# Rotary embedding on one core: batches moved in pairs as 32 KB rows, a lead of one row, another start

## The chip, the cores and the metric

The kernel runs on one core of one Trainium2 chip. Times are device microseconds of the whole execution. The span is the part that the profile covers, from the first instruction to the last; the time is about 1.4 us longer. A run is compared with runs of the kernel before on the same chip and, for the most part, in the same rounds. All ratios are the mean time of one kernel's fast runs over the mean of the other's fast runs, so they are not quite the ratio of the medians quoted beside them. Brackets hold the 95% interval.

## The reference

`x` is 16 batches of 512 rows of 1024 fp32 numbers, a row being 16 heads of 64. Each head is rotated by the row's angles:

```
x1, x2 = x[..., :half_dim], x[..., half_dim:]          # half_dim 32
out = concatenate([x1 * cos - x2 * sin, x1 * sin + x2 * cos], axis=-1)
```

33.55 MB come in and 33.55 MB go out. There is one product with the cosine (t1), one of the swapped halves with the signed sine (t2), and a sum.

## The kernel before

A batch is a tile of 2 MB: 4 rows to each of 128 partitions, so one contiguous run of 16 KB per partition in DRAM. Tiles go through a ring of 40 rows in SBUF. SyncE issues the loads (queue q1), ScalarE the stores (q10). GpSimd computes most t2, VectorE all t1 (into PSUM) and most sums; for three rows in eight, TensorE adds t2 with an identity matmul and ScalarE copies the sum out.

```
RING, LEAD = 40, 2
PE2 = [u % 8 in (1, 3, 6) for u in range(NU)]     # summed by TensorE, copied out by ScalarE
V2 = [u % 8 == 3 for u in range(NU)]              # t2 by VectorE instead of GpSimd
...
xv = x.rearrange("b (p r) d -> b p (r d)", r=R)   # R = 4: 16 KB to a partition
...
# SyncE
for c in range(NC):
    if c * R >= RING:
        sp.wait_ge(sem_out[c - RING // R], 16)
    sp.dma_start(tile(c), xv[c]).then_inc(sem_in[c], 16)
...
# ScalarE
ae.dma_start(out[0, 0:seq:seq // 16, 0, 0:HALF], cos[0:seq:seq // 16, :]).then_inc(sem_touch, 16)   # early write of 2 KB
...
    if r == R - 1:
        if c == 0:
            ae.wait_ge(sem_touch, 16)
        wait_added(ae, u)
        ae.dma_start(ov[c], tile(c)).then_inc(sem_out[c] if c < len(sem_out) else sem_rest, 16)
...
# VectorE: the sum of a row trails its product by LEAD rows
for u in range(NU + LEAD):
    if u < NU:
        mul(u)
    if u >= LEAD and not PE2[u - LEAD]:
        comb(u - LEAD)
```

## Time and profile before

| | before |
|---|---|
| time, median of the first 3 runs | 162.03 us |
| span of the profiled run | 160.6 us |
| packets | 4931, of which 4096 of 16 KB |
| DMA share held by q1 and q10 | 49.6% and 48.9% |
| busy VectorE, GpSimd | 131.6 and 130.5 us |
| last store issued | 153.65 us |

The prediction shows the rows of the page, the windows and the GpSimd timeline. To judge a shorter lead one more view is needed, the groups of VectorE with the waits ahead of them (count, busy us, mean ns; after the last bar the idle time just before, and what ended most of it):

```profile
L229 DVE TENSOR_TENSOR t_ps<-x_sb,tab_ps 128x1024 f32<-128x1024 f32 x64 | 77.3, 1227 | 13.4 <-ACT x_sb L144 11.6
L240 DVE TENSOR_TENSOR x_sb<-t_ps,t_sb 128x1024 f32<-128x1024 f32 x40 | 48.6, 1217 | 0.0
```

VectorE stood still 11.6 us for ScalarE to empty a PSUM buffer. And the timeline of the tail, with the instruction that issues the last store at the end:

```profile
150.07 1.23 DVE L229 TENSOR_TENSOR t_ps<-x_sb,tab_ps 128x1024 f32<-128x1024 f32 x1
...
151.21 2.35 DVE L240 TENSOR_TENSOR x_sb<-t_ps,t_sb 128x1024 f32<-128x1024 f32 x2
152.53 1.02 ACT L144 ACTIVATE x_sb<-t_ps 128x1024 f32<-128x1024 f32 x1 [4.88 <-PE t_ps L169]
153.65 0.34 ACTq L149 DMA_DIRECT2D out_dram<-x_sb  x1
```

The last two sums on VectorE and the copy of row 62, after its detour over TensorE and ScalarE, both ended at 153.55 or 153.56, and the last store was issued 0.1 us later.

### The profile page before, as it was taken

The numbers are of one execution on the slowest core, as the hardware profiler recorded it, in microseconds if no ns is written. First come the engines' busy times: TensorE is split into PE (matmuls) and PEld (weight loads), VectorE is DVE, ScalarE is ACT, GpSimd is POOL, SyncE is SP. The second block draws the span as 40 slices with busy tenths as digits, with TensorE's granted clock in tenths as the row PEclk, the third lists the DMA queues.
The fourth block names the chain that finished last, engine by engine and source line by source line (L and its number), as shares of the span: only waits on it lengthen the run. The fifth ranks groups of instructions, "written<-read, shape, count | busy, mean of one in ns | idle before, by whom it ended". The sixth has DMA issues, their size and how long they took to land.

```text
span 160.6 us, 608 instructions
## 1 busy us (share of the span) xinstructions
PE 85.6 (53%) x102; PEld 26.6 (17%) x102; DVE 131.6 (82%) x116; ACT 26.4 (16%) x27; POOL 130.5 (81%) x62
## 2 busy tenths in 40 slices
PE   6004909358529548538548646756626844545800
PEld 1002302212202202211202211211111210120200
DVE  0079299998899969997899989996999979996920
ACT  3010220220120121121021022022012022202020
POOL 1069999999999999999987997999939989399000
PEclk9999975555855556855556755556755586755585
DMA  4999999999999999999999999999999999999996
GB/s 131 404 457 420 441 432 412 432 420 441 416 445 437 416 441 414 445 428 428 435 420 445 424 428 437 424 437 428 428 437 428 432 432 420 445 428 428 437 416 279
DMA packets 4931, 67.27 MB, mean 419 GB/s; under 512 B 576, under 2 KB 832, under 8 KB 832
## 3 DMA queue, kind: packets, MB, share of 16 engines
q1 hardware_dynamic: 2592, 33.69, 49.6%
q10 hardware_dynamic: 2336, 33.56, 48.9%
q14 instruction: 3, 0.02, 0.0%
HBM read 33.69 MB, written 33.56 MB: 419 GB/s over the span
## 4 chain that ended last, share of the span: by engine, by line
DVE 30%; PE 21%; issue 19%; POOL 15%; ACT 5%; DMA 5%; SPq 0%; DVEq 0%; POOLq 0%
PE t_ps L169 21%; DVE x_sb L240 17%; POOL t_sb L198 15%; DVE t_ps L229 10%; ACT x_sb L144 5%; DMA stage<-in_sin_dram 5%; DVE t_sb L220 3%; SPq L128 0%; SPq L125 0%; ACT s_sb L138 0%; ACT s_sb L139 0%; DVEq L228 0%; DVEq L239 0%; POOLq L117 0%
## 5 line engine op out<-in xcount | busy, mean ns | idle before, releaser
L198 POOL TENSOR_TENSOR t_sb<-x_sb,s_sb 128x1024 f32<-128x1024 f32 x56 | 129.8, 2350 | 17.3 <-ACT s_sb L139 8.2
L169 PE MATMUL t_ps<-t_sb,ident 128*128 128x512 f32 x96 | 82.8, 1015 | 65.7 <-DVE t_ps L229 52.6
L229 DVE TENSOR_TENSOR t_ps<-x_sb,tab_ps 128x1024 f32<-128x1024 f32 x64 | 77.3, 1227 | 13.4 <-ACT x_sb L144 11.6
L240 DVE TENSOR_TENSOR x_sb<-t_ps,t_sb 128x1024 f32<-128x1024 f32 x40 | 48.6, 1217 | 0.0
L169 PEld LDWEIGHTS t_ps<-t_sb,ident 128*128 128x128 f32 x96 | 25.8, 295 | 122.2 <-DVE t_ps L229 87.9
L144 ACT ACTIVATE x_sb<-t_ps 128x1024 f32<-128x1024 f32 x24 | 24.6, 1024 | 119.5 <-PE t_ps L169 119.5
L220 DVE TENSOR_TENSOR t_sb<-x_sb,tab_ps 128x1024 f32<-128x1024 f32 x8 | 9.7, 1210 | 0.0
L207 DVE COPY tab_ps<-stage 128x128 f32<-128x128 f32 x1 | 0.3, 295 | 7.6 <-DMA stage<-in_cos_dram 7.6
L155 PE MATMUL t_ps<-zero 128*128 128x512 bf16 x6 | 2.7, 629 | 1.3 <-DVE zero L203 1.3
L138 ACT ACT_TABLE_LOAD x1 | 1.3, 1283 | 1.5 <-PEq L273 1.5
L138 ACT ACTIVATE s_sb<-stage 128x128 f32<-128x128 f32 x1 | 0.3, 309 | 6.3 <-DMA stage<-in_sin_dram 6.3
L155 PEld LDWEIGHTS t_ps<-zero 128*128 128x128 bf16 x6 | 0.7, 136 | 2.4 <-DVE zero L203 1.2
L203 DVE MEMSET zero<- 128x256 uint32 x1 | 0.3, 272 | 0.9 <-PEq L273 0.9
L180 POOL MEMSET ident<- 128x128 f32 x1 | 0.2, 204 | 0.3 <-POOLq L273 0.3
L182 POOL TENSOR_SCALAR_AFFINE_SELECT ident<-ident 128x128 f32<-128x128 f32 x1 | 0.3, 293 | 0.1
L273 POOL MEMSET const-float32-0.0<- 128x1 f32 x1 | 0.1, 99 | 0.3 <-issue 0.3
L139 ACT ACTIVATE s_sb<-stage 128x128 f32<-128x128 f32 x1 | 0.3, 292 | 0.0
L209 DVE TENSOR_SCALAR tab_ps<-stage 128x128 f32<-128x128 f32 x1 | 0.3, 284 | 0.0
L210 DVE COPY tab_ps<-stage 128x128 f32<-128x128 f32 x1 | 0.3, 283 | 0.0
L273 POOL MEMSET const-bfloat16-1.0<- 128x1 bf16 x1 | 0.1, 102 | 0.0
L273 POOL MEMSET const-uint8-127<- 128x1 uint8 x1 | 0.1, 102 | 0.0
L273 POOL MEMSET const-float32-1.0<- 128x1 f32 x1 | 0.1, 98 | 0.0
## 6 DMA issues: line engine op xcount, KB each, us to landing
x_sb<-in_x_dram SPq DMA_DIRECT2D x16, 2048.0 KB, 54.5
out_dram<-x_sb ACTq DMA_DIRECT2D x16, 2048.0 KB, 16.0
stage<-in_cos_dram SPq DMA_DIRECT2D x1, 64.0 KB, 7.6
stage<-in_sin_dram SPq DMA_DIRECT2D x1, 64.0 KB, 7.3
out_dram<-in_cos_dram ACTq DMA_DIRECT2D x1, 2.0 KB, 6.5
```

The source lines that it names most:

```text
L138: ae.activation(s_sb[:, :, 0, :], sv, COPY, scale=-1.0)
L139: ae.activation(s_sb[:, :, 1, :], sv, COPY).then_inc(sem_s, 1)
L144: ae.activation(xs[:, k, :], t1_ps[:, u % NT1, :], COPY).then_inc(sem_a, 1)
L155: pe.matmul(t1_ps[:, k, b * BANK:(b + 1) * BANK], zero[:, 0:P], zero[:], start=True, stop=True).then_inc(sem_w, 1)
L169: ins = pe.matmul(t1_ps[:, u % NT1, b * BANK:(b + 1) * BANK], ident[:], t2[:, b * BANK:(b + 1) * BANK], start=False, stop=True, skip_group ...
L182: pl.affine_select(out=ident[:], in_=ident[:], compare_op=mybir.AluOpType.is_equal, fill=0.0, base=0, pattern=[[-1, P]], channel_multiplier=1,
L198: pl.tensor_tensor(t2_sb[:, u % NT2, :, :, :], swapped(k), sin_of(s_sb, r), mult).then_inc(sem_p, 1)
L203: ve.memset(zero[:], 0.0).then_inc(sem_z, 1)
L220: ve.tensor_tensor(t2_sb[:, u % NT2, :, :, :], swapped(k), sin_of(s_ps, r), mult).then_inc(sem_d, 1)
L229: ve.tensor_tensor(t1_ps[:, u % NT1, :].rearrange("p (h d) -> p h d", d=HALF), x_sb[:, k, :, :, :].rearrange("p h t d -> p (h t) d"), c_ps ...
L240: ve.tensor_tensor(xs[:, k, :], t1_ps[:, u % NT1, :], t2_sb[:, u % NT2, :, :, :].rearrange("p h t d -> p (h t d)"), add,).then_inc(sem_v, 1)
L273: nc = _bacc.Bacc("TRN2", target_bir_lowering=False, num_devices=1)
```

## The change

The intent is fewer and longer packets. Twelve of the batches move in pairs b and b + 6: partition p holds 8 consecutive rows of one of the two, 32 KB in one run. Two batches at each end stay alone, so that compute starts and ends on small tiles. The pair needs its own cosine and sine tables (two small matmuls with a picking matrix). The lead goes from 2 to 1, three rows at the ends are summed on VectorE instead of TensorE, and two more t2 go to GpSimd. At the start, the first row of the first batch is stored alone, and the early write to `out` is gone.

```diff
-    RING = 40
-    NC = batch
+    FAR = (batch - 4) // 2
+    tiles = [(0, R1), (1, R1)] + [(2 + i, R2) for i in range(FAR)] + [(batch - 2, R1), (batch - 1, R1)]
+    RING = 5 * R2
...
-    PE2 = [u % 8 in (1, 3, 6) for u in range(NU)]
-    V2 = [u % 8 == 3 for u in range(NU)]
+    PE2 = [R1 <= u < NU - R1 and u % R2 in (1, 3, 6) for u in range(NU)]
+    V2 = [tiles[t][1] == R2 and r == V_ROW for t, r in rows]
...
-    LEAD = 2
+    LEAD = 1
...
+        x2 = x.rearrange("b (s r) d -> s b (r d)", r=R2)
+        def in_dram(single, pairs, t, r=0):
+            b, n = tiles[t]
+            return single[b, :, r * dim:] if n == R1 else pairs[:, b:b + FAR + 1:FAR, :]
...
-            ae.dma_start(out[0, 0:seq:seq // 16, 0, 0:HALF], cos[0:seq:seq // 16, :]).then_inc(sem_touch, 16)
...
-                if r == R - 1:
-                    if c == 0:
-                        ae.wait_ge(sem_touch, 16)
+                if u == 0:
                     wait_added(ae, u)
-                    ae.dma_start(ov[c], tile(c)).then_inc(sem_out[c] if c < len(sem_out) else sem_rest, 16)
+                    ae.dma_start(o1[0, :, 0:dim], xs[:, 0, :]).then_inc(sem_out[0], 16)
+                if r == tiles[t][1] - 1:
+                    wait_added(ae, u)
+                    k = u // R2
+                    ae.dma_start(in_dram(o1, o2, t, t == 0), in_sbuf(t, t == 0)).then_inc(sem_out[k] if k < EARLY else sem_rest, 16)
```

## The prediction

> **What bounds the kernel now.** I read the page from the top: which engine is never idle, then what the rest wait for. The busy rows and the DMA queues come first.
>
> ```profile
> span 160.6 us, 608 instructions
> ...
> DMA  4999999999999999999999999999999999999996
> GB/s 131 404 457 420 441 432 412 432 420 441 416 445 437 416 441 414 445 428 428 435 420 445 424 428 437 424 437 428 428 437 428 432 432 420 445 428 428 437 416 279
> DMA packets 4931, 67.27 MB, mean 419 GB/s; under 512 B 576, under 2 KB 832, under 8 KB 832
> ## 3 DMA queue, kind: packets, MB, share of 16 engines
> q1 hardware_dynamic: 2592, 33.69, 49.6%
> q10 hardware_dynamic: 2336, 33.56, 48.9%
> ```
>
> The DMA row is full in every slice but the first and the last. The two queues (q1 loads, q10 stores) together held the 16 engines for 49.6 + 48.9 = 98.5% of the span. No compute engine comes near: VectorE is 82% busy, GpSimd 81%. So the question is the work that the DMA engines have, and the unfilled corners at both ends. The windows view separates corners from middle (the last two columns are the DMA share and GB/s):
>
> ```profile
> 0.00:4.00 4.00, 2.74 (x6) 0.73 (x6) 0.27 (x1) 1.28 (x1) 0.70 (x6) 1.00 0.45 131
> 4.00:24.00 20.00, 5.95 (x8) 2.33 (x8) 12.21 (x14) 2.56 (x4) 14.40 (x7) 0.96 1.01 429
> 24.00:136.00 112.00, 67.18 (x76) 20.48 (x76) 103.08 (x90) 19.46 (x19) 105.72 (x46) 0.58 1.01 430
> 136.00:156.00 20.00, 9.72 (x12) 3.03 (x12) 16.05 (x14) 3.07 (x3) 9.73 (x5) 0.65 1.00 429
> 156.00:160.60 4.60, 0.00 (x0) 0.00 (x0) 0.00 (x0) 0.00 (x0) 0.00 (x0) 0.50 0.71 301
> ```
>
> Loads alone (4 to 24), loads with stores (24 to 136) and stores nearly alone (136 to 156) all run at 429 to 430 GB/s. That equality says the engines' own pace is the limit, not HBM and not the direction. The packet records agree: of the 4096 packets of 16 KB, the median load and the median store both took 611 ns, 26.8 GB/s an engine, 429 on 16.
>
> Is compute a close second? The GpSimd timeline of the last third (start, us, then the wait before in brackets) answers:
>
> ```profile
> 102.73 7.06 POOL L198 TENSOR_TENSOR t_sb<-x_sb,s_sb 128x1024 f32<-128x1024 f32 x3
> 110.05 6.98 POOL L198 TENSOR_TENSOR t_sb<-x_sb,s_sb 128x1024 f32<-128x1024 f32 x3 [0.27 <-DMA x_sb<-in_x_dram]
> 119.78 9.30 POOL L198 TENSOR_TENSOR t_sb<-x_sb,s_sb 128x1024 f32<-128x1024 f32 x4 [2.75 <-DMA x_sb<-in_x_dram]
> 129.49 6.97 POOL L198 TENSOR_TENSOR t_sb<-x_sb,s_sb 128x1024 f32<-128x1024 f32 x3 [0.41 <-DMA x_sb<-in_x_dram]
> 139.21 9.28 POOL L198 TENSOR_TENSOR t_sb<-x_sb,s_sb 128x1024 f32<-128x1024 f32 x4 [2.75 <-DMA x_sb<-in_x_dram]
> ```
>
> From 110 us on GpSimd has caught up and waits for each load. The chain of waits nevertheless names compute (DVE 30%, PE 21%), because it follows the last store back to the sum that fed it. But the last store was issued at 153.65 and its packets ran right behind those of the store before (which ended at 155.1), so the tail had under 1 us of slack and no hole. Compute sets the time only if the change makes that last issue later.
>
> **What the Trainium skill says.** "DMA: Bandwidth & Descriptors", section "Where 436 GB/s comes from": 16 ports of 32 B at 850 MHz, 435.2 GB/s. The trace agrees with that as an asymptote: its packets of 512 B took 27 ns and those of 16384 B 611 ns, so (611 - 27) / 15872 B is 36.8 ps a byte, 27.2 GB/s an engine. The same page, "Why small descriptors are slow (HBM only)", has a fixed cost of some 3 cycles per packet. The trace shows more: 611 - 16384 x 0.0368 = 8.2 ns, and the 4-byte packets took 9 ns by themselves; I use 8.2. Its "Latency and other measured facts" warns of row pitches of large powers of two in HBM (half rate at 4 MiB); the pair's neighbours will be 6 batches, 12 MiB, apart, and no run here shows what that does. Its "The descriptor swizzle" spreads 128 partitions over engines so that each has one memory port; for a pattern of 64 by 2 rows on the DRAM side the page says nothing, and that is my largest doubt.
>
> **The change, part by part.**
>
> 1. *32 KB rows.* Twelve of sixteen batches, three quarters of 4096 packets, go from 16 KB to 32 KB: 3072 packets become 1536. If a 32 KB row is one packet, it takes 32768 x 0.0368 + 8.2 = 1214 ns where two took 1222. Removed per engine: 1536 / 16 x 8.2 ns = 0.79 us, on the bound itself. The bytes stay: 67.1 MB at 435 GB/s is 154.3 us, no version goes below that plus its corners.
> 2. *First row alone.* One store of 2 MB becomes one of 4 KB rows and one of 12 KB rows: 128 packets more, 128 / 16 x 8.2 ns = +0.07 us.
> 3. *No early write to out.* 16 packets of 128 B at 13 ns, one an engine: -0.01 us. Nothing waits visibly for it (it landed in 6.5 us, the first store is issued at 21.8). The first load's packets, up to 1.77 us each, lie beside it; if it disturbed them, up to some 0.7 us might come back (queue 1's mean of 618 ns against 611, times 128 packets per engine, is 0.9 us). I count none.
> 4. *Stores start sooner, then come in lumps of 4 MB.* Row 0 can be summed about 4 us after GpSimd starts at 9.6, so its store is issued near 14 instead of 21.8. Loads filled the engines then anyway: 0. Later, when the store queue is empty, 20 MB of loads stand queued: 0.
> 5. *Work moved between engines.* The order view shows 58 GpSimd products for 56, 43 sums on VectorE for 40, 6 of its own products for 8, 42 matmuls of sums for 48. GpSimd: +2 x 2.35 = +4.7 us, 58 x 2.35 = 136.3 in all. VectorE: 64 + 43 + 6 = 113 instructions for 112, +1.2 us. Neither is on the bound unless the tail slips.
> 6. *Tail.* GpSimd from 9.6 without a stop would end at 145.9. In the kernel before it ended at 148.5 and the last store followed 5.2 us later, since sums trailed by two rows and row 62 went over TensorE (3.5 us) and ScalarE. With a lead of one row and no such detour in the last four rows I allow 2 us. The pair of rows 48 to 55 lands whole, so row 48 comes later: loads end near 138 now, less 4 MB at half rate (19.5 us) gives 118, less what stores in lumps let loads gain early. If compute really starts there at 114 to 118, then 7 + 8 products of 2.35 = 35.3 end at 149 to 153, and the last store is issued at 151 to 155. The deadline from above is 155.1 less the 0.8 us from issue to first packet, 154.3. So expected slack 1 to 3 us, loss expected 0.2.
> 7. *Tables.* Two matmuls, four small copies, three set-up instructions on GpSimd, all before row 8 (near 28 us): 0.
>
> Sum: -0.79 + 0.07 - 0.01 + 0.2 = about -0.5 us on 160.6, hence 160.1. The timed run was 1.4 us above its span (162.04 to 160.6), so 161.5. Since parts 3 and 4 can only give, I shade it to 161.3.
>
> **Rivals.** *Compute becomes the bound at the end.* For: 4.7 us more on GpSimd, whole pairs landing late, sums only one row behind, so VectorE meets GpSimd's latency each row. Against: the lead of two cost waits on ScalarE (11.6 us in 8), since fewer VectorE instructions lay between a product and the reuse of its buffer; a lead of one puts another there. Time if it goes wrong: each us after 154.3 is a us, 162 to 165. *The new pattern runs slower on the engines*, by uneven ports or HBM rows 12 MiB apart: a packet of 1300 ns instead of 1214 costs 96 x 86 ns = 8.3 us, some 170. For: nothing in the profile, only the silence of the skill; against: reads and writes held 611 ns flat in every mixture, so HBM has room. *The rows are cut into 16 KB packets again*: then part 1 is nil, 162.0. *The early write had held up the start*: 160.6.
>
> **Range and chances.** The middle cases span 160.6 to 162.5; the tail rival stretches the upper side, so 160.2 to 163.4. Faster by over 2% means under 158.8: the floor of 154.3 + 1.8 until the first packet + 0.5 after the last + 1.4 is 158.0 with no packet cost and no ragged end, so 0.03. Slower by over 2% needs above 165.3, the engine pattern rival or a badly late tail: 0.09. Within 2%: 0.88.
>
> **What would show it.** Right: some 3,300 packets for 4931, 32 KB ones near 1214 ns, DMA share full from 4 us to the last store, GB/s of 431 to 433 in the middle, the last store issued before 154. Wrong: packets of 32 KB above 1225 ns; a digit under 9 in the DMA row before the last slice (compute late); a first slice well above 131 GB/s (the early write did matter); GpSimd's idle time growing on VectorE instead of on loads.

## The result, and the profile after

The changed kernel took 162.00 us (median of 6 runs, 161.41 to 162.24), the kernel before 162.03: ratio 0.999 [0.9968, 1.0012]. Two repeats gave 0.9997 [0.9979, 1.0015] and 0.9995 [0.9983, 1.0007]. So the forecast gain of about 0.45% did not come. These are the same lines of the page as the prediction shows of the kernel before:

```profile
span 160.8 us, 569 instructions
...
DMA  5999999999899999999999999999999999999994
GB/s 147 403 457 461 426 448 420 390 401 506 363 436 440 467 399 473 424 408 467 424 399 456 448 391 440 473 428 387 493 395 403 428 469 395 489 416 391 440 424 204
DMA packets 3314, 67.26 MB, mean 418 GB/s; under 512 B 368, under 2 KB 624, under 8 KB 752
## 3 DMA queue, kind: packets, MB, share of 16 engines
q1 hardware_dynamic: 1728, 33.69, 49.5%
q10 hardware_dynamic: 1584, 33.56, 48.5%
```

The packets fell from 4931 to 3314 as meant. But q1 and q10 hold the engines for 98.0% of the span, where it was 98.5%, and the last slice moved 204 GB/s where it had moved 279: the work on the engines shrank, and some of it ends later. (The 8 in the DMA row is no hole. A packet that takes 1.2 us is booked as a whole, so neighbouring slices of 4 us gain and lose by it; the packet records have no gap above 15 ns on any engine there.) The windows, with DMA share and GB/s last:

```profile
4.00:24.00 20.00, 2.04 (x4) 1.17 (x4) 14.59 (x14) 1.17 (x4) 14.38 (x7) 1.00 1.03 439
24.00:136.00 112.00, 61.96 (x82) 20.64 (x83) 105.87 (x95) 20.47 (x20) 110.46 (x48) 0.74 1.00 431
136.00:156.00 20.00, 2.53 (x3) 0.44 (x2) 9.43 (x8) 1.02 (x1) 9.27 (x4) 0.59 0.98 421
156.00:160.80 4.80, 0.00 (x0) 0.00 (x0) 0.00 (x0) 0.00 (x0) 0.00 (x0) 0.50 0.57 246
```

The long middle gained, 431 GB/s for 430. The last window lost: a share of 0.57 over 4.80 us, where the kernel before had 0.71 over 4.60. Compute is not the cause. VectorE's group with its wait, and the tail of the timeline:

```profile
L296 DVE TENSOR_TENSOR t_ps<-x_sb,pair_ps 128x1024 f32<-128x1024 f32 x48 | 57.6, 1222 | 2.9 <-ACT x_sb L177 2.9
```

```profile
109.17 25.46 POOL L260 TENSOR_TENSOR t_sb<-x_sb,s_sb 128x1024 f32<-128x1024 f32 x11 [0.17 <-DMA x_sb<-in_x_dram]
138.39 9.27 POOL L260 TENSOR_TENSOR t_sb<-x_sb,s_sb 128x1024 f32<-128x1024 f32 x4 [3.76 <-DMA x_sb<-in_x_dram]
```

```profile
147.77 1.23 DVE L307 TENSOR_TENSOR x_sb<-t_ps,t_sb 128x1024 f32<-128x1024 f32 x1 [1.08 <-POOL t_sb L260]
149.08 0.34 ACTq L185 DMA_DIRECT2D out_dram<-x_sb  x1
```

The wait for ScalarE fell from 11.6 to 2.9 us, GpSimd waits for loads and not for VectorE, and the last store is issued at 149.08, 4.6 us earlier than before. It then stands behind other stores.

So who ends late? In the packet records every transfer ends with 16 packets of 4 bytes, one on each DMA engine. Sorted by time, these packets of the last store show every engine's own end. "Middle" is the median of the 16, "last" the sixteenth:

| kernel | middle engine, us | last engine, us | last minus middle |
|---|---|---|---|
| before | 159.51 | 160.12 | 0.61 |
| after | 158.78 | 160.44 | 1.66 |
| after, first repeat | 158.83 | 160.32 | 1.49 |
| after, second repeat | 158.78 | 160.33 | 1.55 |

The middle engine gained 0.7 us, and the last one lost 0.2 to 0.3. (The mean of the sixteen went from 159.61 to 159.00, 159.07 and 158.96.) The time goes by the last. These are three executions with spans of 160.7 and 160.8; of the 17 runs of the changed kernel two had a span of 160.0, and no trace caught one of those. Where it fell behind can be read in the packet records of the first repeat, by putting packets into 16 back-to-back chains. All extra times here are over what a packet of that length usually takes:

```
engine that ended at 160.32, its packets out of the ordinary:
 55.9 us  queue 14 (instructions), 8 KB, 309 ns, between two data packets
 56.2 us  q1  32 KB  +530 ns  (right behind the instruction packet)
122.1 us  q10 32 KB  +158 ns
125.9 us  q10 32 KB  +490 ns
```

0.31 + 0.53 + 0.16 + 0.49 = 1.49 us, all of its lag. Two kinds of events add up: an instruction fetch that passes through one of the 16 data engines, and some slow packets, near 125 us here; in the two other traces the same engine also had one 440 to 540 ns too long at 95 us.

### The profile page after: what moved, and what is told of

Its sections match the earlier page's. It is cut to its first block, busy times and chain, and to the rows that moved or that the text cites. A ratio compares the mean times of both kernels' runs of the same rounds, so it can differ in the third digit from the quotient of the medians.

```text
span 160.8 us, 569 instructions
## 1 busy us (share of the span) xinstructions
PE 69.3 (43%) x94; PEld 23.0 (14%) x94; DVE 130.2 (81%) x117; ACT 23.9 (15%) x26; POOL 136.4 (85%) x67
## 2 busy tenths in 40 slices
DMA packets 3314, 67.26 MB, mean 418 GB/s; under 512 B 368, under 2 KB 624, under 8 KB 752
## 4 chain that ended last, share of the span: by engine, by line
POOL 25%; PE 21%; DVE 16%; issue 15%; DMA 11%; ACT 3%; SPq 1%; POOLq 0%; DVEq 0%
POOL t_sb L260 25%; PE t_ps L215 21%; DMA x_sb<-in_x_dram 11%; DVE t_ps L296 9%; DVE x_sb L307 7%; ACT x_sb L177 3%; SPq L158 1%; DVE t_sb L289 1%; SPq L161 1%; POOLq L145 0%; POOLq L147 0%; DVEq L306 0%
## 5 line engine op out<-in xcount | busy, mean ns | idle before, releaser
L260 POOL TENSOR_TENSOR t_sb<-x_sb,s_sb 128x1024 f32<-128x1024 f32 x58 | 134.1, 2364 | 10.5 <-ACT s_sb L168 6.5
L215 PE MATMUL t_ps<-t_sb,ident 128*128 128x512 f32 x84 | 64.5, 919 | 62.9 <-POOL t_sb L260 41.4
L296 DVE TENSOR_TENSOR t_ps<-x_sb,pair_ps 128x1024 f32<-128x1024 f32 x48 | 57.6, 1222 | 2.9 <-ACT x_sb L177 2.9
L307 DVE TENSOR_TENSOR x_sb<-t_ps,t_sb 128x1024 f32<-128x1024 f32 x43 | 52.4, 1219 | 2.7 <-POOL t_sb L260 2.5
L177 ACT ACTIVATE x_sb<-t_ps 128x1024 f32<-128x1024 f32 x21 | 21.5, 1024 | 106.2 <-PE t_ps L215 106.2
L215 PEld LDWEIGHTS t_ps<-t_sb,ident 128*128 128x128 f32 x84 | 21.1, 278 | 105.4 <-issue 57.2
L296 DVE TENSOR_TENSOR t_ps<-x_sb,tab_ps 128x1024 f32<-128x1024 f32 x16 | 19.3, 1222 | 4.7 <-DMA x_sb<-in_x_dram 4.7
L289 DVE TENSOR_TENSOR t_sb<-x_sb,tab_ps 128x1024 f32<-128x1024 f32 x6 | 7.3, 1213 | 0.0
L198 PE MATMUL pair_ps<-stage,pick 128*128 128x256 f32 x4 | 2.0, 666 | 5.1 <-DMA stage<-in_sin_dram 5.1
L241 POOL TENSOR_SCALAR_AFFINE_SELECT pick<-pick 128x128 f32<-128x128 f32 x2 | 1.4, 704 | 0.1
```

The costliest lines, as they stand in the source:

```text
L177: ae.activation(xs[:, k, :], t1_ps[:, u % NT1, :], COPY).then_inc(sem_a, 1)
L198: pe.matmul(pair_ps[:, k].rearrange("p c r d -> p (c r d)"), pick[:, k].rearrange("q s b -> q (s b)"), stage[:].rearrange("q c f -> q (c f)"),
L215: ins = pe.matmul(t1_ps[:, u % NT1, b * BANK:(b + 1) * BANK], ident[:], t2[:, b * BANK:(b + 1) * BANK], start=False, stop=True, skip_group ...
L241: pl.affine_select(out=pick[:, k], in_=pick[:, k], compare_op=mybir.AluOpType.is_equal, fill=0.0, base=-k, pattern=[[-2, P // 2], [0, 2]], ...
L260: pl.tensor_tensor(t2_sb[:, u % NT2, :, :, :], swapped(k), over_heads(s_of(t, r)), mult).then_inc(sem_p, 1)
L289: ve.tensor_tensor(t2_sb[:, u % NT2, :, :, :], swapped(k), over_heads(v_ps), mult)
```

## The experiments

There were fifteen runs, all with correct results. The first four asked which part of the change moved the time, the next four what the packets cost and what makes an engine late, the rest looked mostly at the start.

### The changed kernel again

No edit.

> The changed kernel once more, unaltered, for a second trace and five more rounds. In the first trace the DMA work per engine fell by 0.63 us (packet times of both queues summed, 158.19 to 157.56 us), yet the last of the 16 engines ended at 160.45 us against 160.13. Theory S (the slowest engine sets the time, and the change spreads the engines): ratio again 0.997 to 1.001, and the last engine again over 1.2 us behind the middle of the 16. Rival L (that trace's slow engine was bad luck): last engine within 0.8 us of the middle, span near 160.1, ratio 0.995 to 0.997.

162.01 us, ratio 0.9997 [0.9979, 1.0015]; mean span of its runs 160.53. It confirms the result, and its trace the picture of a middle engine that gained and a last one that did not.

### Pairs, but 16 KB rows

```diff
-                sp.dma_start(in_sbuf(t), in_dram(x1, x2, t)).then_inc(sem_in[t], 16)
+                for h in range(tiles[t][1] // R1):
+                    sp.dma_start(in_sbuf(t, h * R1, R1), in_dram(x1, x2, t, h * R1, R1)).then_inc(sem_in[t], 16)
```

(and the same for the stores; the waits on a tile count both halves.)

> The changed kernel with each pair's load and store cut into two transfers of 16 KB rows; layout, tables, order and compute stay. It undoes the packet size alone. If the packet saving reaches the end of the kernel, it is slower than the changed kernel by 1536 / 16 x 8.2 ns = 0.8 us (ratio to before 1.003 to 1.005). If the saving is swallowed by the spread of the engines that large packets bring (S), it is the same within 0.3 us and its engines end closer together (under 0.9 us). The packets of a pair's halves should take 611 ns.

163.18 us, 1.0061 [1.0039, 1.0083]. This number misleads: the mean span is 160.70, only 0.1 above that of the kernel before in the same rounds (160.57). The rest lies outside the span. In four of six runs the time was 2.4 to 3.0 us above the span instead of 1.4 or so; the profiled one has a 16 KB packet of a queue that is not the kernel's, at 162.5 us, after the last store. So I compare spans. Middle 159.49, last 160.31, lag 0.82: with 16 KB rows the gain of the middle engine is gone, and so is the large lag.

### Everything but the pairs

The kernel before with a lead of one, the moved rows, no early write and the first row stored alone.

```diff
-    LEAD = 2
+    LEAD = 1
...
-            ae.dma_start(out[0, 0:seq:seq // 16, 0, 0:HALF], cos[0:seq:seq // 16, :]).then_inc(sem_touch, 16)
...
+                if u == 0:
+                    wait_added(ae, u)
+                    ae.dma_start(ov[0][:, 0:dim], xs[:, 0, :]).then_inc(sem_out[0], 16)
```

> The kernel before with all of the change but the pairs: lead of one row, no early write, first row alone, the same rows on TensorE and VectorE, 16 batches of 16 KB rows. If these other parts cost time (rival O), ratio to before 1.003 or more. If they are neutral, ratio 0.999 to 1.002 (arithmetic: +0.07 us of packets). If the early write or the late last store had cost something, it gains: 0.995 to 0.998.

162.06 us, 1.0006 [0.9993, 1.002]; middle 159.62, last 160.42. These parts gain nothing alone.

### The changed kernel with a lead of two

```diff
-    LEAD = 1
+    LEAD = 2
```

> The changed kernel with sums trailing by two rows again. In the changed kernel the last store was issued at 149.1 us, some 4.5 us before it had to be, so by all theories that hold DMA for the bound it stays within 0.5 us of the changed kernel, although the last store moves later by 2 to 5 us. If it is over 1 us slower, compute is closer to the bound than the trace says, and the lead of one pays for the extra GpSimd work.

163.14 us, 1.0056 [1.0034, 1.0078], mean span 161.55. I had expected it within 0.5 us of the changed kernel, and that missed. The windows of the tail (DMA share and GB/s last), the last store, and VectorE's wait for ScalarE (us, times, longest):

```profile
136.00:150.00 14.00, 6.35 (x9) 1.85 (x8) 12.51 (x12) 3.07 (x3) 12.11 (x6) 0.73 0.90 384
150.00:156.00 6.00, 0.00 (x0) 0.00 (x0) 5.38 (x5) 0.00 (x0) 0.00 (x0) 0.54 0.82 350
```

```profile
151.94 3.48 DVE L307 TENSOR_TENSOR x_sb<-t_ps,t_sb 128x1024 f32<-128x1024 f32 x3
155.50 0.34 ACTq L185 DMA_DIRECT2D out_dram<-x_sb  x1
```

```profile
DVE t_ps L296 <- ACT x_sb L177: 12.1, 8, 3.7
```

The store is issued at 155.50, after the engines have run dry (shares of 0.90 and 0.82), and all sixteen then end within 0.16 us of each other, the last at 161.42. Fifteen of them also stood idle for 1 to 2.3 us from 139.1 us on, before the packets of the third-last store (issued at 140.04). That is what a bound by compute looks like: late together, with holes before. It is the prediction's tail rival, 1 us dear. It is VectorE that is late: GpSimd's last product ends at 148.1 us, near the changed kernel's 147.7, but VectorE waits 12.1 us for ScalarE instead of 2.9, and its last sum ends at 155.42. So the lead of one is no gain over the kernel before; in the changed kernel it keeps VectorE's last sums off the bound. Whether the pairs or the moved rows bring them so close to it, no run separates.

### Pairs of neighbouring batches

```diff
-    tiles = [...] + [(2 + i, R2) for i in range(FAR)] + [...]
+    tiles = [...] + [(2 + 2 * i, R2) for i in range(FAR)] + [...]
-            return ... else pairs[:, b:b + FAR + 1:FAR, :]
+            return ... else pairs[:, b:b + 2, :]
```

> The changed kernel with neighbouring batches as pairs (2 MiB apart in DRAM) instead of 12 MiB apart; all else stays. In three traces with 32 KB stores some packets of lagging engines took 75 to 620 ns too long near 122 to 126 us (and 441 near 95 us), none in the traces with 16 KB rows. If that is a matter of DRAM addresses (theory D), the slow packets go or move, and so does the span: 159.7 to 160.1 if they go, ratio near 0.996. If it belongs to large packets as such (theory P), they stay, span 160.3 to 160.7, ratio 0.998 to 1.001.

162.06 us, 1.001 [0.9994, 1.0027]. The two batches of a pair are 2 MB apart instead of 12, and it makes no difference. Slow packets near 125 us are there too (412 and 311 ns extra), so the distance is not their cause. But they fell on other engines than the first fetch, and this trace, of the quickest of the six runs (161.45, the others 161.92 to 162.62), has a lag of 0.60 only. The lag is thus not the same in every execution.

### One more instruction fetch

150 waits that are already fulfilled, on SyncE, so that its program is longer.

```diff
+            for _ in range(150):
+                sp.wait_ge(sem_in[0], 16)
```

> The changed kernel with 150 satisfied waits more on SyncE after its last load is issued: they cost no one time by themselves, but make that engine's instruction stream long enough to be fetched once more in mid-kernel. In every trace so far, the last of the 16 DMA engines is the one that served an instruction fetch near 56 to 63 us (queue 14, 309 ns, and the data packet right behind it took 530 to 576 ns longer). If the fetches set the end (theory F), one more falls near 100 us: on the same engine, the span grows by 0.5 to 0.9 us; on another engine, that one ends some 0.8 us behind the middle and the span stays within 0.2. If fetches are harmless, nothing changes and the fetched engine is not among the last three.

162.12 us, 1.0007 [0.9992, 1.0021], mean span 160.72. The trace has a third packet of queue 14, at 104.4 us. It took 318 ns, the data packet behind it 418 ns longer than usual, and its engine ended last, at 160.12, just after the engine of the first fetch. So a fetch does push an engine back, but one added on another engine cost the kernel little: 0.2 us of mean span (160.72 for 160.53), within the spread of the runs.

### Loads of 32 KB, stores of 16 KB

The store part of the second experiment alone.

> The changed kernel with 32 KB rows for the loads alone; each pair's store is cut into two of 16 KB rows. By packet arithmetic 768 / 16 x 8.2 ns = 0.4 us more than the changed kernel for the middle engine (159.2). If the slow packets near 125 us come with 32 KB stores, they vanish here, the last engine is 0.85 us behind the middle and the span is 160.0 to 160.3, slightly under both kernels. If they don't, 160.6 to 161.

163.76 us, 1.0112 [1.0088, 1.0135], mean span 161.97 (part of the time again lies outside the span). I had expected a span of 160.0 to 160.3, so this missed. The load queue ran empty from 101 to 103.5 us, and the engine with the first fetch had slow packets from 104 to 117 us (up to 620 ns extra); middle 159.11, last 161.49. Why the queues' shares moved: the Trainium skill, "DMA: Bandwidth & Descriptors", section "Queues, rings and completion order", has each engine go round its queues a whole packet at a time. The records agree, if one record is one packet. One engine of the changed kernel, where its load queue held 32 KB rows and its store queue 16 KB rows, started

```
42.31 q10 16 KB   42.92 q1 32 KB   44.13 q10 16 KB   44.73 q1 32 KB   45.94 q10 16 KB
```

So a longer row on one queue gives that queue more of the bytes, here two thirds to the loads. Loads run ahead, fill the ring, and wait.

### The kernel before with 8 KB rows

```diff
-                sp.dma_start(tile(c), xv[c]).then_inc(sem_in[c], 16)
+                for h in range(2):
+                    sp.dma_start(tile(c, h), xv[c][:, h * 2 * dim:(h + 1) * 2 * dim]).then_inc(sem_in[c], 16)
```

(the same for the stores.)

> The kernel before with each load and store cut into two of 8 KB rows: the other direction, 4096 packets more. By 8.2 ns a packet the middle engine ends 4096 / 16 x 8.2 = 2.1 us later, near 161.6, each packet taking 309 ns. If the time follows the packets at all, span 162.3 to 162.7 and ratio 1.011 to 1.013; if packet cost were hidden (pipelined), ratio within 1.003.

163.45 us, 1.0091 [1.0075, 1.0106], below the 1.011 to 1.013 that 8.2 ns per packet gave. This measures the disputed cost by itself: 4096 packets more, 256 an engine, moved the middle engine from 159.51 to 160.71, 1.2 us, or 4.7 ns a packet.

The records say where the other 3.5 ns are. A packet of 16 KB is recorded with 611 ns, but the next on its engine starts 3 to 4 ns before that ends. The pace shows it (landings are those of the middle engine): three stores of the kernel before, alone on the engines, landed at 144.72, 149.59 and 154.45, 4.865 us for 8 packets, 608 each. In the changed kernel loads and stores of 32 KB alternate, and loads landed at 67.91, 87.27 and 106.65: 19.37 us for 16 packets, 1210.6 each, recorded as 1213. The kernel before needs 9.72 us for 16 packets there, 607.5. So a pair saves 2 x 607.5 - 1210.6 = 4.4 ns, with the stores' pace (2 x 608.1) 5.6; about 5. Ninety-six pairs an engine save 0.48 us.

### GpSimd waits for a load once per tile

```diff
-                pl.wait_ge(sem_in[t], 16)
+                if r == 0:
+                    pl.wait_ge(sem_in[t], 16)
```

> The changed kernel with GpSimd waiting for a load at a tile's first row alone (the later waits were satisfied by it): some 44 instructions fewer on GpSimd, the same work. If a fetch comes when an engine's stream reaches a fixed place (its 65th to 70th recorded instruction; GpSimd was at its 70th at the 309 ns packet of 73 us), that packet moves to 110 to 130 us and the one at 56 us (VectorE at its 64th) stays. The span stays 160.3 to 160.8, since the engine that pays for the first fetch still ends last. If the packet stays at 73 us, the fetches are not GpSimd's.

161.81 us, 0.9988 [0.9971, 1.0004]. The second instruction packet moved from 74 to 108.1 us, just short of where I had put it, and the lag fell to 1.13 us in this trace. The interval includes no gain at all.

### The old start

The changed kernel with the early write back, and the first batch stored in one piece.

```diff
-            return (k == 0) + sum(u // R2 == k for u in first)
+            return sum(u // R2 == k for u in first)
+            ae.dma_start(out[0, 0:seq:seq // 16, 0, 0:HALF], cos[0:seq:seq // 16, :]).then_inc(sem_touch, 16)
-                if u == 0:
-                    wait_added(ae, u)
-                    ae.dma_start(o1[0, :, 0:dim], xs[:, 0, :]).then_inc(sem_out[0], 16)
-                    ae.dma_start(in_dram(o1, o2, t, t == 0), in_sbuf(t, t == 0)).then_inc(...)
+                    if t == 0:
+                        ae.wait_ge(sem_touch, 16)
+                    ae.dma_start(in_dram(o1, o2, t), in_sbuf(t)).then_inc(...)
```

> The changed kernel with the start of the kernel before: the early write to out is back, the first batch is stored whole. If these parts are neutral, as the step of the prediction has it (0.06 us), span within 0.2 of the changed kernel's 160.5 (ratio to before 0.998 to 1.001) and the last engine again 1.2 us or more behind the middle. If the slower packets near 23 to 35 us of the kernels without the early write (0.30 to 0.47 us per engine against 0.22) are due to its absence, the middle engine gains 0.1 to 0.2 us.

161.47 us, 0.9964 [0.9952, 0.9976]. This was the first run with a gain clear of noise: middle 158.97, last 159.65, lag 0.67. The start, which I had counted at 0.06 us, decides.

### The kernel before without its early write

The early write and the wait for it are taken out, nothing else.

> The kernel before without its early write, nothing else: the same question from the other side. Neutral: ratio 0.999 to 1.001. If the absence costs: slower first stores, packets of 16 KB near 25 us longer in sum than 0.22 us per engine, ratio 1.001 to 1.003. Its last engine should stay 0.6 to 0.9 us behind the middle, as with all 16 KB rows.

161.95 us, 0.9992 [0.998, 1.0004]: within noise. The early write cost nothing and gained nothing there.

### Which half of the start: the first batch whole, or the early write

First the changed kernel with its first batch stored whole and no early write:

> The changed kernel with its first batch stored in one piece again, and still no early write. The old start (early write and whole first batch) gained 0.57 us over the kernel before: a ratio of 0.9964, against 0.9985 to 1.0 of the changed kernel. Theory A, the first row stored alone is what costs: its store begins 17.7 us into the run instead of about 27, as packets of 4 KB and 12 KB, and shifts all that follows; then this run reads 0.996 to 0.9975, and the last engine ends under 1 us behind the middle one. Theory B, the early write is what helps (its write opens the path to out before the bulk): then this run reads 0.999 to 1.001, like the changed kernel.

161.40 us, 0.9963 [0.995, 0.9975]; middle 159.05, last 159.49, lag 0.44. Its page shows the fuller end, 307 GB/s in the last slice (204 in the changed kernel), and its tail of the timeline shows that this is not compute, since the last store is issued later than in the changed kernel:

```profile
DMA  5999999999999999999999999999999999999997
GB/s 152 401 443 479 402 402 439 463 451 402 393 455 447 467 395 402 475 434 404 451 426 426 443 410 459 402 443 430 398 471 455 418 422 398 492 402 434 434 398 307
DMA packets 3170, 67.26 MB, mean 421 GB/s; under 512 B 352, under 2 KB 608, under 8 KB 608
...
q1 hardware_dynamic: 1728, 33.69, 49.7%
q10 hardware_dynamic: 1440, 33.56, 48.8%
```

```profile
156.00:159.90 3.90, 0.00 (x0) 0.00 (x0) 0.00 (x0) 0.00 (x0) 0.00 (x0) 0.50 0.71 302
```

```profile
151.28 0.34 ACTq L181 DMA_DIRECT2D out_dram<-x_sb  x1
```

The last window has the share of the kernel before, 0.71, and it is 0.70 us shorter. Then the early write back, with the first row still alone:

> The changed kernel with the early write put back, and its first row still stored alone. Theory A (the row alone costs): 0.999 to 1.001, with the last engine 1.1 us or more behind the middle one. Theory B (the early write helps): 0.996 to 0.9975. In the kernel before, taking the early write away moved nothing (0.9992), which speaks for A.

161.65 us median, 0.9994 [0.9967, 1.002]. Four runs lay at 161.5 to 161.7, two at 162.2 and 163.0; the profiled one is a quick one (161.52), with a lag of 0.90, where the theory of the row alone had asked for 1.1 or more. On the mean this is the changed kernel again, as that theory had it, but the interval holds the other theory's 0.997 too; the run is not of one piece, and whether the early write helps some executions stays open.

The changed kernel on the same chip:

> The changed kernel once more, for the comparison within one chip: 0.9985 to 1.0005, its slowest engine 1.1 to 1.7 us behind the middle one.

161.96 us, 0.9995 [0.9983, 1.0007]; middle 158.78, last 160.33. Its interval does not touch that of the whole first batch, nor do the runs themselves (161.72 to 162.12, and 161.34 to 161.51). **So storing the first row alone costs about 0.5 us** (162.0 against 161.4, mean spans 160.52 and 160.00), and it costs it in the spread of the engines, not in their work: the mean of the sixteen ends is 158.96 here and 158.94 with the batch whole. In the ten traces with 32 KB rows both ways and a lead of one, the engine that served the first fetch ends last or within 0.05 us of the last, with the batch whole too.

### The old start with fewer waits on GpSimd

> The old start, with GpSimd's wait for the load made once per tile and not once per row. Each of the two gained alone (0.9964 and 0.9988). If the second is a gain of its own (it moves a fetch of instructions from 74 us to 108 us and nothing else that I see), this reads 0.995 to 0.996; if it was spread of the runs, 0.996 to 0.997.

161.69 us, 0.9985 [0.9965, 1.0004]: three runs at 161.4, three at 161.95 to 162.3. Both forecasts missed. The fewer waits bring no gain of their own, so nothing speaks for one in the 0.9988 above; and the whole first batch does not give 161.4 in every execution.

### Two answers side by side

The runs fill a small table, with ratios to the kernel before:

| | first batch stored whole | first row stored alone |
|---|---|---|
| 16 KB rows | 0.9992 (no early write) | 1.0006 (everything but the pairs) |
| 32 KB rows | 0.9963 | 0.9995 to 0.9997; first runs 0.999 |

The columns of the first line also differ in the lead and the moved rows. With the first batch whole, the rows of 32 KB are worth 0.0029 x 162 = 0.47 us, near the 0.48 us of the packets, though the intervals leave about 0.2 to 0.75. With the row alone most of that is lost again.

Why a start at 13 us should spread the engines at 125 us is **not settled**. Two facts stand beside each other. In the kernel with the old start, from 50 us on, every pair of loads ends with a pair of stores, within 0.3 us (loads 71.45, 90.82 and 110.25, stores 71.56, 91.12 and 110.52); in the changed kernel they are out of step (loads 67.91, 87.27 and 106.65, stores 75.12, 94.50 and 112.12). And slow packets of 380 to 490 ns near 125 us are in all three traces of the changed kernel, while the three with the batch whole have none there above 152 ns. But the run with the row alone and the early write has none either. Nor does the step decide alone: that run and the one of neighbouring batches are out of step too (loads 87.9 and 87.5, stores 94.5 both), with lags of 0.90 and 0.60, and the old start with fewer waits is in step, but its traced run ended at 160.1 because its middle engine was late (159.46). I have no run that sets the step of the two queues by itself.

## Why the prediction was right or wrong

The bound was right. The sixteen DMA engines are full from 4 us to the end, compute stays hidden, and the time moved by less than 2%. The forecast sum of -0.5 us failed, in two terms.

*32 KB rows, -0.79 us.* The mechanism held: 3314 packets, those of 32 KB at a median of 1213 ns (1214 forecast). The size was off. The 8.2 ns came from recorded durations of packets, and these overlap by 3 to 4 ns. The pace of landings gives about 5 ns, so -0.48 us, and the run with 8 KB rows 4.7 ns. ("The trace shows more" than the skill's 3 cycles was no comparison, since that section gives no time for a cycle.)

*First row alone, +0.07 us.* This is the step that failed most. I counted 8 packets an engine and no more. Measured: 0.5 us (0.9995 against 0.9963 on one chip). The sum took all engines as one, but the end is set by the slowest of them, and in the three traces of the changed kernel it ended 1.5 to 1.7 us behind the middle one, for 0.6 in the kernel before and 0.45 with the batch whole. How the row makes it so stays open.

*No early write, -0.01.* Right: 0.9992 [0.998, 1.0004] without it in the kernel before. The 0.7 us that "might come back" do not. The first slice rose from 131 to 147 GB/s, which the text named as a sign that the write matters; it was a false sign. The first slice also reads 147 to 160 in four traces that have the early write, and 134 in one that has not (lead of two), so it varies without it.

*Stores sooner, 0.* Not so simple: nothing is seen lost at the start itself, but the step of loads and stores is another from there to the end. Whether that is the way to the 0.5 us is not shown.

*Work moved, and the tail, +0.2 us.* The tail was easier than forecast: 149.08 for "151 to 155". GpSimd began the last pair at 109.17 and not at 114 to 118, and only the 4 products of the last tile then waited for a load by more than 0.2 us (3.76). No loss. The rival behind it is real: with a lead of two the same kernel issues at 155.50 and takes 1 us more. One claim about the kernel before was too strong. Its tail was not quite without a hole: seven engines waited 0.08 to 0.42 us for the last store.

*The pattern of 64 by 2 rows* was the largest doubt and is harmless: 1213 ns, and pairs 2 MB apart instead of 12 give 1.001 [0.9994, 1.0027].

Put together: -0.48 + 0.5 + 0 = about 0, where the three ratios (0.999 to 0.9997) say -0.16 to -0.05, none of them clear of no change. That the two terms cancel so nearly is chance. The version without the failed part beats both kernels: pairs with the first batch stored whole, 161.40 us.

## What to carry to other kernels

When all DMA engines are full, look at each engine's own end and not at the mean share: a saving per packet reaches the time only if the slowest engine gets it too. Take the cost of a packet from the pace of landings, since recorded durations can overlap. And try a small "harmless" store by itself: with 32 KB rows, one row stored early cost as much as twelve batches of longer packets gained.

## What the Trainium skill lacked or had wrong

- "DMA: Bandwidth & Descriptors", "Why small descriptors are slow (HBM only)": it names a fixed 3 cycles a packet, without a time. Measured here: about 5 ns of pace (4.7 with 8 KB rows), while recorded durations suggest 8.2. Nor is it said that records of neighbouring packets overlap, by 3 to 4 ns.
- "Runtime: NRT & Kernel Launch", "Instruction fetch mechanics": it calls the cost of a fetch mostly hidden. For the compute engines no run here shows otherwise. But a fetch is a packet of 8 KB in a queue of its own on one of the 16 data engines: it took 309 ns in most cases, and the data packet behind it 80 to 630 ns more (the first fetch mid-kernel about 460 to 630), 0.84 us or so on one engine, which in the traces with 32 KB rows both ways and a lead of one ended last or within 0.05 us of the last.
- No page that I read says how far the slowest of the 16 engines, which ends a transfer, can trail the middle one when all are full: 0.4 to 2.4 us here.
- "DMA: Bandwidth & Descriptors", "The descriptor swizzle": nothing on a DRAM side of 64 by 2 rows. A packet of 32 KB takes 1213 ns there, with neighbours 2 MB or 12 MB apart.
- No page that I read says that the time beyond the span can differ between runs of one kernel: about 1.4 us in most, 2.4 to 3.0 in four of six runs with pairs of 16 KB rows, where the trace has a 16 KB packet of another queue after the last store (1.1 us).
